# Attention scores on the full array: the low half of k stored twice, and the keys laid out anew

## The chip, the cores and the metric

The kernel runs on one core of one Trainium2 chip. The metric is the device time of one execution in microseconds. Before the change the median of three runs is 2488.95 us (2488.07 to 2495.45).

## The reference, cut to what matters

One inference step of a trunk of two layers, over 128 context tokens and 512 latent tokens on an 8 x 64 grid. Each layer has three mixer branches and a gated feed-forward. Two branches are attention, and the change is in how their scores are computed:

```python
def block_attention(q, k, v):              # branch a: 8 query heads, 2 key/value heads, head width 64
    s = jnp.einsum('bqgrd,bkgd->bgrqk', q_i, k).astype(jnp.float32) * scale
    p = jax.nn.softmax(s, axis=-1)
...
def neighbourhood_attention(q, k, v, kc, vc, rpb):   # branch c: 8 heads, 8 x 16 window
    s_loc = jnp.einsum('bqhd,bqkhd->bhqk', q_i, k_i) * scale + bias_i
    s_ctx = jnp.einsum('bqhd,bchd->bhqc', q_i, kc) * scale
    p = jax.nn.softmax(jnp.concatenate([s_loc, s_ctx], axis=-1), axis=-1)
```

Latent queries of branch a see 512 latent and 128 cached keys; those of branch c see their window and 128 cached keys; context queries see the 128 context keys alone. Branch b is a state-space model (S5).

## The kernel before

Products run in a reduced-width float32 format, and each operand is kept as a high part and a low part, so that a product is a sum of three (high x high, high x low, low x high). Dense products of the hidden state stream 384 or 256 tokens over a stationary 128 x 128 block of weights (`fm_run`, `fm_half`), which come as chunks of 512 KB and are split in two parts by the scalar and the vector engine on the way.

**Scores.** A head is 64 wide and the array takes 128 rows. So `stack` and `evac_q` put the high part of q in one half of the partitions and the low part in the other, and k's high part is stored in both halves. One product over 128 rows then gives (q high + q low) x k high. A second product takes only the 64 partitions that hold q's high part, against k's low part, which is stored once (`klo`): this is a matmul on a row tile of the array. The helper is `scores`.

**Branch a (`gqa_prep`, `gqa`, `gqa_unit`).** For each of four pairs of heads and five tiles of 128 queries, the 640 scores of a head lie in two banks of PSUM, as 512 and 128 columns; with two products each, that is four matmuls per head. Context tiles have one run of 128 keys. `softmax` takes the maximum (vector engine), the exponential (scalar engine) and the scaling (vector engine); then the probabilities are transposed (`transpose_P`, tile `PT`) and multiplied by v (`pv`, tile `y`, two column tiles of 64). The dense products of the gates, the S5 outputs, its gated unit and branch b fill the tensor engine meanwhile.

**Branch c (`neighbourhood`, `na_proj`, `na_pair`).** For each pair of heads, `na_proj` projects q and k and `na_pair` works on blocks 0 to 3 of 128 latent queries and block 4, the context. A latent block has 256 window keys, from two neighbouring tiles of 128, and the 128 cached ones: 256 and 128 columns, two products each, four matmuls per head. The bias is added to the window's scores by the vector engine, the cached keys' scores are copied by the scalar engine, both into `Pn`. Fill comes from the projections of the next pair, branch a's output product, gate c and, in layer 0, the modulation products.

**Order.** The tile framework orders each engine's instructions by what can run first in its own simulated timeline (`schedule_with_timeline_sim=True`); what frees banks is marked `top()`. All DMAs of the kernel are issued by the sync engine (SP), in order.

Of the kernel before, what the change touches and what calls it, by code (L numbers as in the profile page):

```python
# [38 lines left out]
# gates before the S5 outputs; gates of branch c among them; chunks of w_in[u] and of w_up split in halves  # L39
# [4 lines left out]
# chunks of w_out and w_down (8 and 22) kept for the later token tiles; the groups of tiles; the order of the chunks  # L44
# [6 lines left out]
class Trunk:  # L51
# [111 lines left out]
    # ------------------------------------------------------------ weight stream  # L163
# [36 lines left out]
    def ws_early(self, first, n, pool):  # L200
        """Chunks ahead of their turn, for products that start with the tokens of the first half."""
# [6 lines left out]
    def ws_next(self, *key):  # L208
        """The hi and lo parts of the next chunk of weights, which the host lays out by the keys asked for."""
# [15 lines left out]
    # ------------------------------------------------------------ matmul groups  # L225
# [6 lines left out]
    def fm_half(self, out, w, a, K, c, n):  # L232
        """out[128 features, n tokens] = sum over k of w[:, k].T @ a[:, k, c:c+n], in hi/lo parts."""
# [26 lines left out]
    def tm_run(self, name, l, kper, n, evac):  # L260
        """Token-major products of the hidden state with n outputs."""
# [15 lines left out]
    # ------------------------------------------------------------ program  # L277
# [22 lines left out]
    def extra(self):  # L300
        """Three more banks, while the wide scores don't need them."""
# [24 lines left out]
    def setup(self):  # L326
# [20 lines left out]
        # silu of the two conditioning vectors, in the first two of 32 columns  # L347
# [118 lines left out]
    def adaln(self, l, vecs, pool, raw, bank):  # L466
        """silu(c) @ w_mod + b of both conditioning vectors, four tiles of 256 columns side by side on the array."""
# [60 lines left out]
    def tails(self, outs, xt, nxt):  # L528
        """x += gg * rmsnorm(product) of the token tiles; then the norm nxt = (layer, which), or the output."""
# [91 lines left out]
    def out_phase(self, name, K, src, l, which, nxt):  # L621
        """x += gg * rmsnorm(product), and the norm that follows, over groups of token tiles. Of w_out most chunks stay
        for the later groups, and the third tile goes between the others, so that the first three are normed in time
        for the next phase."""
# [47 lines left out]
    # ------------------------------------------------------------ mixer  # L672
# [62 lines left out]
    def gates(self, l, pool):  # L735
        """Gate b, which stays in M, and what of the other two gates is done early and kept in DRAM."""
# [50 lines left out]
    def nv(self, l, VN):  # L787
        """The values of the neighbourhood attention, token-major."""
# [8 lines left out]
    def gate(self, l, b, dst, js=range(8)):  # L797
        """tanh of half the gate logits of one branch."""
# [8 lines left out]
    def br(self, l, b, y, G=None):  # L807
        """merged (times 2) += 2 * sigmoid(gate logits) * (y @ w_br) of one branch; the first finds its gate in M."""
# [17 lines left out]
    # ------------------------------------------------------------ attention  # L826
    def scores(self, out, q, k, klo, r0, qv, kv):
        """q.T @ k of one head: q is stacked (hi at r0, lo in the other half), k is hi twice, klo at r0."""
        self.mm(out, qv(q), kv(k), True, False)
        self.mm(out, qv(q[r0:r0 + 64]), kv(klo[r0:r0 + 64]), False, True)  # L830

    def transpose_P(self, parts, pool, npt):
        """The [128, 128] parts of probabilities, transposed; four at a time."""
# [11 lines left out]
    def softmax(self, P, src, nk):  # L845
        """exp(src - max), divided by its sum, of two heads."""
        m, sm, r = (self.st([128, 2], x) for x in ("mx", "sm", "rc"))
        for hh in range(2):
            c = slice(hh, hh + 1)
            self.nc.vector.tensor_reduce(out=m[:, c], in_=src[hh], axis=AX.X, op=ALU.max, negate=True)  # L850
            self.act(P[:, hh, :nk], src[hh], AF.Exp, bias=m[:, c], accum=sm[:, c])
# [3 lines left out]
    def pv(self, tiles, pt, v):  # L855
        """probabilities.T @ v of two heads side by side on the array."""
# [13 lines left out]
    def gqa_prep(self, l, pool, p_y, zt):  # L870
# [7 lines left out]
        ckt = tab[:, 4, 384:512]  # L878
        self.dma(g.rearrange("p a d -> p (a d)"), A["qkg"][l].to_broadcast([128, 128]))
        kst = self.kst = pool.tile([128, 3, 768], R, tag="kst", name="kst")  # L880
        self.dma(ckt, A["ckt"][l])
# [28 lines left out]
        klo = kst[:, 2]  # L910
        parts = [(x[:, :n], c, n) for x, c, n in b] + [(ckt, 640, 128)]
        for b, c, n in parts:
            for kv in range(2):
                r = slice(kv * 64, kv * 64 + 64)
                for o in (0, 64):
                    self.act(kst[o:o + 64, kv, c:c + n], b[r])
                self.sub(klo[r, c:c + n], b[r], kst[r, kv, c:c + n].bitcast(F))
# [10 lines left out]
    def stack(self, pool, zt, p):  # L928
        """q of the two heads of pair p, stacked hi/lo, times 1/8."""
# [10 lines left out]
    def gqa_unit(self, pool, p_sc, p, t, q, va):  # L940
        """Two query heads of one pair, 128 queries: softmax over 640 keys (latents) or 128 (context)."""
        kv = p // 2
        k, klo = self.kst[:, kv], self.kst[:, 2]
# [3 lines left out]
        for hh in range(2):  # L947
            sc.append(p_sc.tile([128, 1024], F, tag="sc", name="sc"))
            for a, b in ((0, 512), (512, 640)) if t else ((0, 128),):
                c0 = a + (128 if t else 0)  # L950
                self.scores(sc[hh][:, a:b], q[:, hh], k, klo, 64 * kv, qv, lambda x: x[:, c0:c0 + b - a])
        P = pool.tile([128, 2, 640], F, tag="P", name="P", bufs=2)
        self.softmax(P, [x[:, :nk] for x in sc], nk)
# [5 lines left out]
    # ------------------------------------------------------------ neighbourhood attention  # L959
# [25 lines left out]
    def na_pair(self, pool, yc, p, ops):  # L985
        """Two heads, 128 queries: blocks 0..2 are grid columns 8+16b.., block 3 the outer 8 + 8 columns, 4 the context."""
        q, kk, bias, _, _ = ops
        k, klo = (kk[:, 0], kk[:, 1]), kk[:, 2]
        for b in (4, 0, 1, 2, 3):
# [4 lines left out]
            def kv(x):  # L994
                if b == 3:
                    return x[:, 128:640].rearrange("p (u v) -> p u v", v=128)[:, 0::3, :]
                return x[:, 128 + 128 * b:384 + 128 * b]

            P = pool.tile([128, 2, 384], F, tag="P", name="Pn", bufs=2)
            for hh in range(2):  # L1000
                sc = self.tq() if (5 * hh + b) % 3 == 0 else self.px()
                if b < 4:
                    self.scores(sc[:, 0:256], q[hh], k[hh], klo, hh * 64, qv, kv)
                c0 = 0 if b == 4 else 640
                self.scores(sc[:, nk - 128:nk], q[hh], k[hh], klo, hh * 64, qv, lambda x: x[:, c0:c0 + 128])
                if b < 4:
                    v = lambda x: x.rearrange("p (g r c) -> p g r c", g=4, r=8)
                    bb = bias[:, hh, 1 if b == 3 else 0, :].rearrange("p (r g c) -> p g r c", r=8, g=4)
                    self.add(v(P[:, hh, 0:256]), v(sc[:, 0:256]), bb)
                self.act(P[:, hh, nk - 128:nk], sc[:, nk - 128:nk])  # L1010
# [3 lines left out]
            tiles = {4: [0], 3: [1, 4, 5]}.get(b, [b + 1, b + 2, 5])  # L1014
# [8 lines left out]
    def na_bias(self, l):  # L1023
        """Relative bias of the two kinds of query block, laid out by query: [128, 8 heads, 8 rows x 32 columns]."""
# [554 lines left out]
```

## Time and profile before

| | |
|---|---|
| runs | 2488.07, 2488.95, 2495.45 us |
| span of the profiled execution | 2490.8 us |
| tensor engine busy | 2430.1 us (98%), 16154 matmuls |
| weight loads busy | 2140.1 us (86%) |
| vector engine busy | 1483.9 us (60%) |
| scalar engine busy | 1229.6 us (49%) |
| mean granted clock of the tensor engine | 0.991 |

The profile gives no time for its execution apart from the span, which lies 1.9 us above the median of the runs. Matmuls overlap in their pipeline and their ends are modelled: a matmul's duration reads about 0.16 us longer than the distance to the next one's start. What a matmul costs is therefore read from start to start in the timeline. A line of the timeline joins neighbouring instructions of one name, shows the shape of the first, and xN is their count; "128\*128" is rows x columns of the array that are used, "64\*128" is a row tile, "128x384" is rows x streamed columns.

### The profile page before, as it was taken

The page shows a single profiled execution, that of the slowest core. Times are in us where ns is not written, and L with a number is a line of the kernel's source. Part 1 is how long each engine was busy: PE and PEld are TensorE (multiplying, and loading weights), DVE is VectorE, ACT ScalarE, POOL GpSimd, SP SyncE. Part 2 cuts the span into 40 slices and gives each one's busy share as a digit, 9 for nine tenths or more (in the row PEclk, how much of TensorE's full clock was granted, in tenths as well). Part 3 has the DMA queues.
Part 4 walks back from the last instruction along what each step waited for, and adds up shares of the span by engine and source line. Part 5 has one row for each costly group of instructions (what it writes and reads, how often), then busy time and mean ns, then how long its engine had stood idle before and what let it go on. Part 6 is the DMA issues. An engine that isn't in the chain of part 4 may idle for free.

```text
span 2490.8 us, 41473 instructions
## 1 busy us (share of the span) xinstructions
PE 2430.1 (98%) x16154; PEld 2140.1 (86%) x16154; DVE 1483.9 (60%) x3269; ACT 1229.6 (49%) x2679; POOL 0.7 (0%) x6
## 2 busy tenths in 40 slices
PE   5999999999999999999999999999999999999998
PEld 4888887878788888999888988888888899999886
DVE  8788536355456866665474684463654665444446
ACT  5434675345536544344465447754455364444434
POOL 0000000000000000000000000000000000000000
PEclk8999999999999999999999999999999999999999
DMA  7862342444224567654456313413211432222335
GB/s 262 276 209 80 107 142 57 138 133 152 86 90 147 193 218 229 215 174 142 156 189 197 106 60 121 134 47 120 86 50 53 147 121 89 73 72 77 127 110 178
DMA packets 158510, 333.91 MB, mean 134 GB/s; under 512 B 38954, under 2 KB 71530, under 8 KB 158314
## 3 DMA queue, kind: packets, MB, share of 16 engines
q1 hardware_dynamic: 158314, 331.26, 40.7%
q8 instruction: 127, 2.08, 0.4%
q14 instruction: 69, 0.57, 0.1%
HBM read 288.05 MB, written 52.53 MB: 137 GB/s over the span
## 4 chain that ended last, share of the span: by engine, by line
PE 93%; DMA 2%; ACT 2%; DVE 2%; issue 1%; SPq 0%; DVEq 0%; ACTq 0%
PE mm L227 52%; PE m L227 16%; PE mx L227 9%; PE tq L227 4%; PE sc L227 3%; PE y L227 3%; PE PT L230 3%; DMA wm<-in_wmod 1%; PE E L227 1%; DMA ar<-in_wmod 1%; PE BT L230 1%; DMA raw<-in_wst 0%; PE xT L230 0%; DVE lo L99 0%; ACT h L130 0%
## 5 line engine op out<-in xcount | busy, mean ns | idle before, releaser
L227 PE MATMUL mm<-h,hi 128*128 128x384 f32 (+1 forms) x3808 | 866.1, 315 | 7.2 <-ACT h L130 4.1
L227 PEld LDWEIGHTS mm<-h,hi 128*128 128x128 f32 x3808 | 642.6, 190 | 29.8 <-issue 15.9
L227 PE MATMUL mm<-h,lo 128*128 128x384 f32 (+1 forms) x1904 | 594.7, 312 | 0.0
L99 DVE TENSOR_TENSOR lo<-raw,hi 128x1024 fp32r<-128x1024 f32 x294 | 359.6, 1224 | 309.8 <-ACT hi L130 307.0
L130 ACT ACTIVATE hi<-raw 128x1024 fp32r<-128x1024 f32 x294 | 310.9, 1058 | 311.9 <-PE mm L227 214.0
L227 PEld LDWEIGHTS mm<-h,lo 128*128 128x128 f32 x1904 | 361.8, 190 | 4.7 <-issue 3.7
L227 PE MATMUL m<-h,hi 128*128 128x256 f32 (+1 forms) x1120 | 250.8, 313 | 1.8 <-ACT vn L130 1.1
L227 PEld LDWEIGHTS m<-h,hi 128*128 128x128 f32 x1120 | 188.4, 190 | 8.0 <-issue 4.6
L227 PE MATMUL m<-h,lo 128*128 128x256 f32 (+1 forms) x560 | 174.3, 311 | 0.1
L130 ACT ACTIVATE PT<-PT 128x512 f32<-128x512 f32 (+1 forms) x176 | 87.0, 499 | 122.0 <-PE PT L230 97.2
L117 DVE SCALAR_TENSOR_TENSOR c<-u,blob,c 128x641 f32<-128x641 f32 x156 | 137.9, 884 | 2.2
L227 PEld LDWEIGHTS m<-h,lo 128*128 128x128 f32 x560 | 106.3, 190 | 2.7 <-issue 2.2
L130 ACT ACTIVATE u<-mm 128x256 f32<-128x256 f32 (+1 forms) x156 | 48.1, 344 | 113.0 <-PE mm L227 113.0
L227 PE MATMUL sc<-kst,qst 64*128 64x128 f32 (+3 forms) x288 | 96.6, 387 | 0.0
L227 PE MATMUL mm<-a,hi 128*128 128x384 f32 (+1 forms) x384 | 89.9, 321 | 2.1 <-DVE a L117 1.3
L227 PEld LDWEIGHTS sc<-kst,qst 128*128 128x128 f32 (+1 forms) x288 | 53.3, 185 | 40.5 <-issue 33.9
L850 DVE TENSOR_REDUCE mx<-sc 128x1 f32<-128x640 f32 (+1 forms) x80 | 57.2, 716 | 44.7 <-PE sc L227 44.1
L130 ACT ACTIVATE HK<-a 64x32 f32<-64x32 f32 (+1 forms) x256 | 77.2, 335 | 12.8 <-PE mm L227 10.3
L227 PE MATMUL mm<-hi,sph 128*128 128x512 f32 x208 | 78.5, 392 | 1.4 <-ACT sph L130 1.4
L227 PE MATMUL mm<-lo,sph 128*128 128x512 f32 x208 | 78.5, 391 | 0.0
L99 DVE TENSOR_TENSOR pr<-PW,cS 128x576 f32<-128x576 f32 x64 | 47.8, 754 | 51.4 <-PE mx L227 32.3
L227 PE MATMUL mm<-set,hi 128*128 128x384 f32 (+1 forms) x324 | 76.6, 320 | 0.3 <-DVE a L117 0.3
(357 smaller groups left out, 4393.6 us busy)
## 6 DMA issues: line engine op xcount, KB each, us to landing
raw<-in_wst SPq DMA_DIRECT2D x308, 512.0 KB
ar<-in_wmod SPq DMA_DIRECT2D x80, 512.0 KB
cd<-pr SPq DMA_DIRECT2D x32, 288.0 KB
v<-cd SPq DMA_DIRECT2D x32, 288.0 KB
wm<-in_wmod SPq DMA_DIRECT2D x8, 1024.0 KB
xd<-xt SPq DMA_DIRECT2D x15, 512.0 KB
xt<-xd SPq DMA_DIRECT2D x15, 512.0 KB
bd<-BT SPq DMA_DIRECT2D x28, 256.0 KB
```

Of the source, the lines that this page charges most:

```text
L99: return self.nc.vector.tensor_tensor(out=out, in0=a, in1=b, op=op)
L117: self.nc.vector.scalar_tensor_tensor(out=out, in0=a, scalar=s, in1=b, op0=op0, op1=op1)
L130: return self.nc.scalar.activation(out=out, in_=a, func=func, **kw)
L227: return self.nc.tensor.matmul(out=out, lhsT=lhsT, rhs=rhs, start=start, stop=stop)
L230: return self.nc.tensor.transpose(out, in_, self.ident)
L850: self.nc.vector.tensor_reduce(out=m[:, c], in_=src[hh], axis=AX.X, op=ALU.max, negate=True)
```

## The change

The low part of k is stored in both halves of the partitions, as the high part is, so that both products of a score go over 128 rows. (The second product then adds q low x k low too.) The 640 keys of a latent tile in branch a are taken as two runs of 320, one per bank. In branch c the cached keys stand twice among the latent ones, at columns 384 and 768, so that the 384 keys of any block are one run (block 3: three pieces at a stride), with one matmul per product; v's tiles are taken in the same order, and the bias add of blocks 1 and 3 is cut in two because the cached keys stand in the middle. The cached keys are loaded by four DMAs instead of one, into both halves; in branch a they land in a part of the table that also serves as scratch for the rotary, and later in the program. The softmax reads the scores of branch a as two runs of 320. The tiles grow, and a scratch size of the program is lowered (every DMA of this kernel goes by SP's queue).

```diff
-    def scores(self, out, q, k, klo, r0, qv, kv):
+    def scores(self, out, q, k, klo, qv, kv):
         self.mm(out, qv(q), kv(k), True, False)
-        self.mm(out, qv(q[r0:r0 + 64]), kv(klo[r0:r0 + 64]), False, True)
+        self.mm(out, qv(q), kv(klo), False, True)
...
# gqa_prep
-        ckt = tab[:, 4, 384:512]
+        ck2 = tab[:, 4, 0:256].rearrange("p (a k) -> p a k", a=2)
-        kst = self.kst = pool.tile([128, 3, 768], R, tag="kst", name="kst")
-        self.dma(ckt, A["ckt"][l])
+        kst = self.kst = pool.tile([128, 4, 768], R, tag="kst", name="kst")
...
         b = self.transposed(zt, 512, self.tq)
-        klo = kst[:, 2]
-        parts = [(x[:, :n], c, n) for x, c, n in b] + [(ckt, 640, 128)]
-        for b, c, n in parts:
+        for kv in range(2):
+            for o in (0, 64):
+                self.dma(ck2[o:o + 64, kv], A["ckt"][l][kv * 64:kv * 64 + 64])
+        for b, c, n in b:
             for kv in range(2):
                 r = slice(kv * 64, kv * 64 + 64)
                 for o in (0, 64):
-                    self.act(kst[o:o + 64, kv, c:c + n], b[r])
-                self.sub(klo[r, c:c + n], b[r], kst[r, kv, c:c + n].bitcast(F))
+                    hi, lo = (kst[o:o + 64, i + kv, c:c + n] for i in (0, 2))
+                    self.act(hi, b[r, :n])
+                    self.sub(lo, b[r, :n], hi.bitcast(F))
+        hi, lo = (kst[:, i:i + 2, 640:768] for i in (0, 2))
+        self.act(hi, ck2)
+        self.sub(lo, ck2, hi.bitcast(F))
...
# gqa_unit
-            for a, b in ((0, 512), (512, 640)) if t else ((0, 128),):
-                c0 = a + (128 if t else 0)
-                self.scores(sc[hh][:, a:b], q[:, hh], k, klo, 64 * kv, qv, lambda x: x[:, c0:c0 + b - a])
+            for a, c0, n in ((0, 128, 320), (512, 448, 320)) if t else ((0, 0, 128),):
+                self.scores(sc[hh][:, a:a + n], q[:, hh], k, klo, qv, lambda x: x[:, c0:c0 + n])
...
# na_pair
+                self.scores(sc[:, 0:nk], q[hh], kk[:, hh], kk[:, 2 + hh], qv, kv)
+                cc = 0 if b == 4 else 128 if b % 2 else 256
                 if b < 4:
-                    self.scores(sc[:, 0:256], q[hh], k[hh], klo, hh * 64, qv, kv)
-                c0 = 0 if b == 4 else 640
-                self.scores(sc[:, nk - 128:nk], q[hh], k[hh], klo, hh * 64, qv, lambda x: x[:, c0:c0 + 128])
...
+                    for c0, g0, ng in ((0, 0, 2), (256, 2, 2)) if b % 2 else ((0, 0, 4),):
+                        v = lambda x: x[:, c0:c0 + 64 * ng].rearrange("p (g r c) -> p g r c", g=ng, r=8)
+                        self.add(v(P[:, hh]), v(sc), bb[:, g0:g0 + ng])
...
# na_proj
-        self.dma(ckt, self.A["cknt"][l, p])
+        for hh in range(2):
+            for o in (0, 64):
+                self.dma(ck2[o:o + 64, hh], self.A["cknt"][l, p][hh * 64:hh * 64 + 64])
...
+            c += 128 * half
             for hh in range(2):
-                r, o = slice(hh * 64, hh * 64 + 64), slice(64 - hh * 64, 128 - hh * 64)
-                self.act(k[hh][r, c:c + n], src[r])
-                self.act(k[hh][o, c:c + n], src[r])
-                self.sub(klo[r, c:c + n], src[r], k[hh][r, c:c + n].bitcast(F))
...
+                for o in (0, 64):
+                    hi, lo = (kk[o:o + 64, i + hh, c:c + n] for i in (0, 2))
+                    self.act(hi, ps[hh * 64:hh * 64 + 64])
+                    self.sub(lo, ps[hh * 64:hh * 64 + 64], hi.bitcast(F))
...
-                put_k(ckt, 640, 128)
+                for c in (384, 768):
+                    hi, lo = (kk[:, i:i + 2, c:c + 128] for i in (0, 2))
+                    self.act(hi, ck2)
+                    self.sub(lo, ck2, hi.bitcast(F))
```

## Rows read from the trace of the kernel before

**Rows 1.** The page: span, busy time of each engine, chain by engine.

```profile
span 2490.8 us, 41473 instructions
PE 2430.1 (98%) x16154; PEld 2140.1 (86%) x16154; DVE 1483.9 (60%) x3269; ACT 1229.6 (49%) x2679; POOL 0.7 (0%) x6
...
PE 93%; DMA 2%; ACT 2%; DVE 2%; issue 1%; SPq 0%; DVEq 0%; ACTq 0%
```

**Rows 2.** Windows 205:455, 500:745, 1440:1710 and 1735:1965, summed.

```profile
sum 995.00, PE 981.99 PEld 838.72 DVE 560.78 ACT 534.37 POOL 0.00; mean PE 245.50 PEld 209.68 DVE 140.20 ACT 133.59 POOL 0.00
```

**Rows 3.** Timeline of PE: four scores of branch a, dense on both sides.

```profile
413.07 1.33 PE L227 MATMUL sc<-kst,qst 128*128 128x512 f32 x4
414.34 0.50 PE L227 MATMUL mm<-a,hi 128*128 128x256 f32 x2
414.68 0.28 PE L227 MATMUL mm<-a,lo 128*128 128x256 f32 x1
```

**Rows 4.** Timeline of PE: eight scores of branch c, two heads of a block.

```profile
525.13 1.10 PE L227 MATMUL mx<-set 128*128 128x256 f32 x4
...
527.30 0.44 PE L227 MATMUL mm<-set,hi 128*128 128x384 f32 x1
527.58 0.34 PE L227 MATMUL mm<-set,lo 128*128 128x384 f32 x1
```

**Rows 5.** Timeline of PE: scores of a context tile, two heads.

```profile
250.34 1.09 PE L227 MATMUL sc<-kst,qst 128*128 128x128 f32 x4
251.36 0.44 PE L227 MATMUL mm<-h,lo 128*128 128x384 f32 x1
```

**Rows 6.** Timeline of PE: dense products without a break.

```profile
2203.31 0.51 PE L227 MATMUL mm<-h,hi 128*128 128x384 f32 x2
...
2207.48 0.40 PE L227 MATMUL mm<-h,hi 128*128 128x256 f32 x2
...
2210.34 0.52 PE L227 MATMUL m<-h,hi 128*128 128x384 f32 x2
```

**Rows 7.** Timeline of PE: single scores among dense products, full and row-tiled.

```profile
1801.85 0.22 PE L227 MATMUL mx<-set 128*128 128x128 f32 x1
1801.91 0.39 PE L227 MATMUL m<-h,hi 128*128 128x384 f32 x1
1802.13 0.33 PE L227 MATMUL m<-h,lo 128*128 128x384 f32 x1
...
1802.66 0.34 PE L227 MATMUL m<-h,lo 128*128 128x384 f32 x1
1802.93 0.32 PE L227 MATMUL mx<-set 64*128 64x128 f32 x1
1803.18 0.61 PE L227 MATMUL m<-h,hi 128*128 128x384 f32 x2
1803.63 0.34 PE L227 MATMUL m<-h,lo 128*128 128x384 f32 x1
```

**Rows 8.** Timeline of the weight loads: the first row tile of Rows 3.

```profile
413.40 0.18 PEld L227 LDWEIGHTS sc<-kst,qst 64*128 64x128 f32 x1 [0.31 <-issue]
```

**Rows 9.** The page's groups: weight loads of the dense products.

```profile
L227 PEld LDWEIGHTS mm<-h,hi 128*128 128x128 f32 x3808 | 642.6, 190 | 29.8 <-issue 15.9
```

**Rows 10.** Groups by form on DVE: operations of the kinds that the change adds.

```profile
L99 DVE TENSOR_TENSOR set<-mm,set 64x384 fp32r<-64x384 f32 x16 | 8.9, 555 | 16.5 <-ACT set L130 16.2
L99 DVE TENSOR_TENSOR set<-mm,set 64x256 fp32r<-64x256 f32 x12 | 5.0, 419 | 1.7 <-ACT set L130 1.5
L99 DVE TENSOR_TENSOR set<-sf,set 64x128 fp32r<-64x128 f32 x16 | 4.5, 283 | 1.9 <-ACT set L130 1.4
```

**Rows 11.** Window in which layer 1's q and k of branch a are prepared.

```profile
1410.00:1445.00 35.00, 35.00 (x241) 34.87 (x240) 31.99 (x102) 15.02 (x34) 0.00 (x0) 1.00 0.25 78
```

**Rows 12.** What the SP queue waited for longest: us in total, times, longest.

```profile
SPq L136 <- DVE lo L99: 858.6, 188, 19.7
```

**Rows 13.** Tile sf: issues of the cached keys, ns min/median/max.

```profile
L136 SPq DMA_DIRECT2D sf<-in_cknt x8: 327/328/424, 483.5 to 1832.0; - x8
```

More of the change, by code (lines that the diff above doesn't have):

```diff
@@ L849, in softmax @@
             c = slice(hh, hh + 1)
-            self.nc.vector.tensor_reduce(out=m[:, c], in_=src[hh], axis=AX.X, op=ALU.max, negate=True)
-            self.act(P[:, hh, :nk], src[hh], AF.Exp, bias=m[:, c], accum=sm[:, c])
+            wide = len(src[hh].shape) == 3
+            self.nc.vector.tensor_reduce(out=m[:, c], in_=src[hh], axis=AX.XY if wide else AX.X, op=ALU.max, negate=True)
+            o = P[:, hh, :nk]
+            self.act(o.rearrange("p (b c) -> p b c", b=2) if wide else o, src[hh], AF.Exp, bias=m[:, c],
+                     accum=sm[:, c])
             self.nc.vector.reciprocal(out=r[:, c], in_=sm[:, c])
@@ L942, in gqa_unit @@
         kv = p // 2
-        k, klo = self.kst[:, kv], self.kst[:, 2]
+        k, klo = self.kst[:, kv], self.kst[:, 2 + kv]
         nk = 640 if t else 128
@@ L948, in gqa_unit @@
             sc.append(p_sc.tile([128, 1024], F, tag="sc", name="sc"))
-            for a, b in ((0, 512), (512, 640)) if t else ((0, 128),):
-                c0 = a + (128 if t else 0)
-                self.scores(sc[hh][:, a:b], q[:, hh], k, klo, 64 * kv, qv, lambda x: x[:, c0:c0 + b - a])
+            for a, c0, n in ((0, 128, 320), (512, 448, 320)) if t else ((0, 0, 128),):
+                self.scores(sc[hh][:, a:a + n], q[:, hh], k, klo, qv, lambda x: x[:, c0:c0 + n])
         P = pool.tile([128, 2, 640], F, tag="P", name="P", bufs=2)
-        self.softmax(P, [x[:, :nk] for x in sc], nk)
+        self.softmax(P, [x.rearrange("p (b c) -> p b c", b=2)[:, :, :320] if t else x[:, :128] for x in sc], nk)
         pt = self.transpose_P([P[:, hh, kt * 128:kt * 128 + 128] for kt in range(nk // 128) for hh in range(2)], pool, 2)
@@ L987, in na_pair @@
         q, kk, bias, _, _ = ops
-        k, klo = (kk[:, 0], kk[:, 1]), kk[:, 2]
         for b in (4, 0, 1, 2, 3):
@@ L995, in kv @@
                 if b == 3:
-                    return x[:, 128:640].rearrange("p (u v) -> p u v", v=128)[:, 0::3, :]
-                return x[:, 128 + 128 * b:384 + 128 * b]
+                    return x[:, 128:896].rearrange("p (u v) -> p u v", v=128)[:, 0::2, :]
+                c0 = (128, 256, 512, 0, 0)[b]
+                return x[:, c0:c0 + nk]
             P = pool.tile([128, 2, 384], F, tag="P", name="Pn", bufs=2)
@@ L1001, in na_pair @@
                 sc = self.tq() if (5 * hh + b) % 3 == 0 else self.px()
+                self.scores(sc[:, 0:nk], q[hh], kk[:, hh], kk[:, 2 + hh], qv, kv)
+                cc = 0 if b == 4 else 128 if b % 2 else 256
                 if b < 4:
-                    self.scores(sc[:, 0:256], q[hh], k[hh], klo, hh * 64, qv, kv)
-                c0 = 0 if b == 4 else 640
-                self.scores(sc[:, nk - 128:nk], q[hh], k[hh], klo, hh * 64, qv, lambda x: x[:, c0:c0 + 128])
-                if b < 4:
-                    v = lambda x: x.rearrange("p (g r c) -> p g r c", g=4, r=8)
                     bb = bias[:, hh, 1 if b == 3 else 0, :].rearrange("p (r g c) -> p g r c", r=8, g=4)
-                    self.add(v(P[:, hh, 0:256]), v(sc[:, 0:256]), bb)
-                self.act(P[:, hh, nk - 128:nk], sc[:, nk - 128:nk])
+                    for c0, g0, ng in ((0, 0, 2), (256, 2, 2)) if b % 2 else ((0, 0, 4),):
+                        v = lambda x: x[:, c0:c0 + 64 * ng].rearrange("p (g r c) -> p g r c", g=ng, r=8)
+                        self.add(v(P[:, hh]), v(sc), bb[:, g0:g0 + ng])
+                self.act(P[:, hh, cc:cc + 128], sc[:, cc:cc + 128])
             self.softmax(P, [P[:, hh, :nk] for hh in range(2)], nk)
@@ L1013, in na_pair @@
             pt = self.transpose_P([P[:, hh, i * 128:i * 128 + 128] for i in range(n) for hh in range(2)], pool, 3)
-            tiles = {4: [0], 3: [1, 4, 5]}.get(b, [b + 1, b + 2, 5])
+            tiles = ([1, 2, 5], [2, 5, 3], [3, 4, 5], [1, 5, 4], [0])[b]
             o = self.pv(tiles, pt, lambda vt, hh: self.VN[:, vt, (2 * p + hh) * 64:(2 * p + hh) * 64 + 64])
@@ L1037, in na_tiles @@
     def na_tiles(self, i, pool, dt=R):
-        return (pool.tile([128, 3840], R, tag=f"set{i}", name="set"),
-                pool.tile([128, 1280], dt, tag=f"sf{i}", name="sf"))
+        return (pool.tile([128, 4992], R, tag=f"set{i}", name="set"),
+                pool.tile([128, 1408], dt, tag=f"sf{i}", name="sf"))
     def na_operands(self, p, pool):
         t, f = self.na_tiles(p % 2, pool, F)
-        kk = t[:, 0:2304].rearrange("p (i c) -> p i c", i=3)
-        q = [t[:, 2304 + i * 704:3008 + i * 704] for i in range(2)]
-        return q, kk, f[:, 0:1024].rearrange("p (h i k) -> p h i k", h=2, i=2), f[:, 1024:1152], f[:, 1152:1280]
+        kk = t[:, 0:3584].rearrange("p (i c) -> p i c", i=4)
+        q = [t[:, 3584 + i * 704:4288 + i * 704] for i in range(2)]
+        ck2 = f[:, 1024:1280].rearrange("p (h k) -> p h k", h=2)
+        return q, kk, f[:, 0:1024].rearrange("p (h i k) -> p h i k", h=2, i=2), ck2, f[:, 1280:1408]
     def na_parts(self, i, pool):
-        t, f = (x.rearrange("p (i k c) -> p i k c", i=2, c=NT) for x in self.na_tiles(i, pool))
+        t, f = (x[:, :n].rearrange("p (i k c) -> p i k c", i=2, c=NT)
+                for x, n in zip(self.na_tiles(i, pool), (3840, 1280)))
         return lambda k: [t[:, i, k] if k < 3 else f[:, i, 0] for i in range(2)]
     def na_proj(self, l, p, ops):
-        q, kk, bias, ckt, kc = ops
-        k, klo = (kk[:, 0], kk[:, 1]), kk[:, 2]
-        self.dma(ckt, self.A["cknt"][l, p])
+        q, kk, bias, ck2, kc = ops
+        for hh in range(2):
+            for o in (0, 64):
+                self.dma(ck2[o:o + 64, hh], self.A["cknt"][l, p][hh * 64:hh * 64 + 64])
         for kind in range(2):
@@ L1066, in evac_q, with evac_k @@
                     self.stt(q[hh][o, d:d + w], src, 0.125, hi.bitcast(F), ALU.mult, ALU.subtract)
-        def put_k(src, c, n):
+        def evac_k(half, ps, c, n):
+            c += 128 * half
             for hh in range(2):
-                r, o = slice(hh * 64, hh * 64 + 64), slice(64 - hh * 64, 128 - hh * 64)
-                self.act(k[hh][r, c:c + n], src[r])
-                self.act(k[hh][o, c:c + n], src[r])
-                self.sub(klo[r, c:c + n], src[r], k[hh][r, c:c + n].bitcast(F))
-        def evac_k(half, ps, c, n):
-            put_k(ps, c, n)
+                for o in (0, 64):
+                    hi, lo = (kk[o:o + 64, i + hh, c:c + n] for i in (0, 2))
+                    self.act(hi, ps[hh * 64:hh * 64 + 64])
+                    self.sub(lo, ps[hh * 64:hh * 64 + 64], hi.bitcast(F))
             if half == 0:
@@ L1560 @@
     from concourse.bass_utils import run_bass_kernel_spmd
-    nc = bacc.Bacc("TRN2", target_bir_lowering=False, num_devices=1)
+    nc = bacc.Bacc("TRN2", target_bir_lowering=False, num_devices=1, dynamic_dma_scratch_size=1024)
     A = {k: nc.dram_tensor(f"in_{k}", v, F, kind="ExternalInput").ap() for k, v in INS.items()}
```

## Prediction

> **What bounds the kernel now.** I read the page first: the tensor engine (PE) is busy 98% of a span of 2490.8 us and holds 93% of the chain that ended last [rows 1]. An average over stages could hide a stage that waits for something else, so I then read the windows of the four stretches in which attention runs (branch a and branch c, in both layers). Together they last 995 us, and PE is busy in 982 of them, the vector engine (DVE) in 561 and the scalar engine (ACT) in 534 [rows 2]. So in the stretches of the change too, PE is what ends last: 13 us of idle time in all. A busy PE is not yet a PE at its rate, so the third view is the timeline of PE, read from one start to the next, for the price of a product there.
>
> **What a dense product costs.** In an unbroken stretch, 24 products of 384 columns take 2207.48 - 2203.31 = 4.17 us, 174 ns each, and the 24 of 256 columns after them 2.86 us, 119 ns each [rows 6].
>
> **What scores cost now.** Four scores of one head in branch a (512 columns on the full array, 512 on a row tile, 128 full, 128 row-tiled) take 414.34 - 413.07 = 1.27 us, and the two dense products after them 0.34 us where two take 0.24: the group costs 1.37 us [rows 3]. Its 1280 columns would take about 0.58 us at the dense rate. In branch c, two heads of a block (1536 columns) take 2.17 us, and the dense product after them 0.28 us for 0.17: 2.28 us [rows 4]. Two heads of a context tile (512 columns) take 1.02 us [rows 5].
>
> **Why, as far as rows tell.** Two single scores of 128 columns stand between dense products [rows 7]. The full one is over after 0.06 us, and the dense product behind it takes 0.22 us for 0.17: about 0.11 us in all. The row-tiled one takes 0.25 us, the dense product ahead of it 0.27 us for 0.17, the one behind it about 0.10 us too much: 0.45 us. So a matmul of few columns isn't dear; passing into a row tile and out of it is, about 0.34 us for the round trip. The loads agree: ahead of the row tile's weights the load unit stands still 0.31 us, with nothing to wait for but issue [rows 8], whereas dense loads have 29.8 us of idle time over 3808 [rows 9].
>
> The Trainium skill, "TensorEngine Tiling (Array Packing)", section Key Properties, says that changing the tiling mode drains the engine; that is what these rows look like, and the change removes such a passage in every score. By another page the sum comes out otherwise; it is a rival below.
>
> **The sum.** Per layer and pair there are four latent tiles or blocks with two heads each: 2 x 4 x 4 x 2 = 64 head groups in each branch, and 8 context units of two heads in each.
>
> - Branch a: four full products of 320 columns. No row shows 320; it lies between 119 and 174 ns, and I take 147. So 1.37 becomes 0.59 us: -0.78 x 64 = -50 us (bounds -43 and -57).
> - Branch c: four full products of 384 columns for two heads: 2.28 becomes 0.70 us: -1.58 x 32 = -51 us.
> - Context: four full products of 128 columns at 0.06 to 0.11 us: 1.02 becomes 0.34 us: -0.68 x 16 = -11 us.
>
> That is 112 us if each group stood alone between dense products. Not all do: groups of different heads already run into each other, and a group followed by a transpose or by a product with v has no cheap neighbour to make cheap again. I take off 10 us, an estimate (bounds 0 and 25): 102 us.
>
> **What it adds.** On DVE, per pair in branch c: two more subtractions of 64x384 and two of 64x256, 2 x 0.555 + 2 x 0.419 = 1.95 us; for the cached keys two of 256 columns in place of two of 128, +0.27 us [rows 10]. Eight pairs: 18 us. The cut bias add is two operations of 128 columns for one of 256, +0.15 us in two blocks, two heads, eight pairs: 5 us. Preparing branch a's keys takes two more subtractions of 512 columns, about 0.69 us each by the step between 256 and 384 [rows 10], and two of 128, less one operation on the cached keys: some 2 us in each layer, 4 in all. So DVE has about 27 us more work; ACT has a little less (one operation for four on branch a's cached keys, two for four in branch c). In the four stretches DVE then has some 588 of about 893 us, 66%, for 56% now: PE's dense products hide it. Without that cover it costs up to 27 us. Two places have thin cover. One is the preparation of branch a in layer 1, where DVE is busy 31.99 of 35 us while PE runs without a gap [rows 11]; gates are the cover, and all 4 us would show without them. The other is the evacuation of k's projection: its bank is held by four subtractions where there were two, 1.1 us longer, with the next-but-one product waiting for it.
>
> **DMAs.** The cached keys are four issues for one: at 0.33 us each [rows 13], 1 us more of SP's time in ten places, and twice as many bytes of a small transfer. In branch a these loads now wait for the rotary's scratch to be free, which they didn't, and weight chunks queue behind them on SP. SP mostly waits for buffers anyway (858.6 us for the weight splits, 19.7 us the longest [rows 12]), and three chunks are split ahead, each worth 24 x (0.174 + 0.119) = 7.0 us of PE [rows 6]. I cost it at nothing; it costs 0 to 10 us. The scratch size, the order of v's tiles and the three-piece keys of block 3 I cost at nothing: same bytes, same counts.
>
> **What is late next.** With scores shorter, each unit's softmax chain starts earlier, but its maximum, exponential, scaling and transposes are as long as before, and fill is used up by the microsecond that the scores no longer take. PE's 13 us of idle time in these stretches [rows 2] should grow. I add 8 us, about two thirds of what is there; from below it is 0, from above about the added DVE work, 27 us.
>
> Sum: 2490.8 - 102 + 8 = 2397 us of span. The median of the runs lies 1.9 us under the profiled span, so the forecast is **2395 us**.
>
> **Rivals.**
> 1. *Waits eat a part* (20%): DVE's 27 us land on PE's path, through banks of k's projection and softmax chains, and the fill that the planner sets aside for the end of a branch is used up too early, about one chunk of 7 us in each of two branches and two layers. 2395 - 8 + 27 + 28 - 2 = about 2440; in part, 2410 to 2440. For it: DVE at 32 of 35 us in one stretch [rows 11]. Against it: 434 us of idle DVE in the four stretches [rows 2].
> 2. *Loads of the full array don't hide* (3%): each of the 448 new products shows its weight load of 190 ns [rows 9] beyond its columns. 448 x 0.19 = 85 us come back: 2480. The Trainium skill, "TensorE: Matmul & The Clock Gate", Part 3, states such a rule: loads overlap matmuls in flight only where the row group differs, which speaks against leaving row tiles. The trace disagrees with it: dense products on all rows go at 119 ns with loads of 190 ns [rows 6, 9], and the load that does not overlap is the row tile's [rows 8].
> 3. *The row tile isn't the cause* (2%): a score keeps its gap of about 0.2 us because of its operands. Branch a keeps its time, as it keeps its four products; in branch c four matmuls become two, 64 x 2 x 0.2 = 26 us: 2463. The lone full score at 0.06 us speaks against it [rows 7].
> 4. *The SP queue* (3%), slower than before: the late loads of cached keys hold up the weight stream behind them in branch a's preparation and at each projection. Ten places; the gain of 94 us is gone once each stops PE for 9.4 us, so from waits of 21 + 9.4 = 30 us on, three chunks being ahead. At 31 us each: 2395 + 104 = 2499. Against it: SP's longest wait is 19.7 us [rows 12].
>
> **How the numbers follow.** The forecast's own case has 72%, with 2376 to 2410: a gain of 112 us and no new waits gives 2377, and 25 us of neighbours that stay dear gives 2410. To hold 8 in 10, the range takes in the part of rival 1 up to 2435: 2377 to 2435, about 15 to 20% left out at both ends. A difference of 0.3%, 7.5 us, is about what a measurement of this kernel can tell from none. Faster: the forecast, rivals 1, 2 (2480 is 0.36% under 2488.95) and 3, less a tail: 95%. Slower: rival 4, 3%. Within 0.3%: 2%.
>
> **What would show it.** In the profile after: no row-tiled score; scores of branch a as four products in 0.59 us between dense ones, of branch c as 174 ns each; no 0.31 us of idle load unit ahead of them; 128 matmuls fewer; PE's busy time down by about 100 us with its share near 97 or 98%; DVE's busy time up by about 27. It would be wrong if full products of scores stood more than about 0.2 us apart, or if idle time of PE rose by tens of microseconds in the four stretches, with DVE or a weight chunk as what ended it.

## The result, and the profile after

The changed kernel takes 2423.75 us, median of four runs (2418.54 to 2427.51), against 2489.18 us (2488.07 to 2495.45): a ratio of 0.9734, 95% interval 0.9717 to 0.9750. It is faster by 65 us where 94 were forecast, and lies inside the range.

The page of the profile after, to be held against [rows 1]:

```profile
span 2416.8 us, 41307 instructions
...
PE 2334.5 (97%) x16026; PEld 2103.6 (87%) x16026; DVE 1501.8 (62%) x3339; ACT 1221.7 (51%) x2657; POOL 0.7 (0%) x6
...
PE 85%; DMA 4%; ACT 4%; DVE 3%; issue 1%; SPq 0%; DVEq 0%; ACTq 0%
```

The tensor engine has 128 matmuls fewer and is busy 2430.1 - 2334.5 = 95.6 us less. But the span fell by only 74.0 us, because the time in which that engine is not busy grew from 2490.8 - 2430.1 = 60.7 to 82.3 us. Its share of the chain fell from 93% to 85%. The clock is not the reason: its mean granted value is 0.990 in this execution, for 0.991 before.

The scores themselves cost what the sum said. Timeline of PE, eight scores of branch a (two heads, 320 columns each) between dense products, to be held against [rows 3]:

```profile
220.88 1.34 PE L227 MATMUL sc<-kst,qst 128*128 128x320 f32 x8
222.06 0.28 PE L227 MATMUL mm<-h,hi 128*128 128x256 f32 x1
222.17 0.28 PE L227 MATMUL mm<-h,lo 128*128 128x256 f32 x1
```

From 220.88 to 222.06 is 1.18 us for eight, 147 ns each, and the dense product behind them takes 0.11 us, no more than its usual 0.12. Timeline of PE, two heads of a block in branch c, to be held against [rows 4]: first between dense products, then behind four transposes.

```profile
1706.86 0.52 PE L227 MATMUL mx<-set 128*128 128x384 f32 x2
1707.21 0.51 PE L227 MATMUL tq<-set 128*128 128x384 f32 x2
1707.56 0.28 PE L227 MATMUL m<-set,hi 128*128 128x256 f32 x1
...
1782.39 0.65 PE L230 MATMUL PT<-ident,Pn 128*128 128x128 f32 x4
1782.81 0.59 PE L227 MATMUL tq<-set 128*128 128x384 f32 x2
1783.24 0.51 PE L227 MATMUL mx<-set 128*128 128x384 f32 x2
1783.59 0.28 PE L227 MATMUL mm<-h,lo 128*128 128x256 f32 x1
```

The first four take 0.70 us, 174 ns each; the ones behind transposes take 0.78. A passage stays, then, of about 0.08 us behind a transpose. It is of the kind for which the forecast took 10 us off. The loads of eight scores now run without a gap (timeline of the weight loads, to be held against [rows 8]):

```profile
220.76 1.19 PEld L227 LDWEIGHTS sc<-kst,qst 128*128 128x128 f32 x8
```

What is new is idle time. The windows over the four stretches of attention after, to be held against [rows 2]:

```profile
205.00:455.00 250.00, 242.71 (x1816) 222.97 (x1815) 150.59 (x416) 154.96 (x376) 0.00 (x0) 0.99 0.33 108
465.00:695.00 230.00, 215.20 (x1533) 182.78 (x1532) 139.28 (x330) 108.35 (x285) 0.00 (x0) 0.98 0.37 123
1410.00:1650.00 240.00, 232.46 (x1746) 214.79 (x1745) 145.32 (x392) 153.61 (x371) 0.00 (x0) 0.99 0.31 102
1660.00:1870.00 210.00, 206.22 (x1446) 188.19 (x1445) 137.03 (x321) 117.09 (x302) 0.00 (x0) 1.00 0.24 75
sum 930.00, PE 896.59 PEld 808.73 DVE 572.22 ACT 534.00 POOL 0.00; mean PE 224.15 PEld 202.18 DVE 143.05 ACT 133.50 POOL 0.00
```

The columns after the length are PE, PEld, DVE, ACT and POOL, busy us and instructions. The tensor engine stands still 33 us of 930, where it was 13 of 995; the largest part, 14.8 us, is in branch c of layer 0. The view of waits names who ended the waits that are new or longer, over the whole program (us in total, times, longest):

```profile
PE m L227 <- DMA ar<-in_wmod: 6.6, 7, 1.5
...
PE y L227 <- ACT PT L130: 4.2, 7, 1.1
PE sc L227 <- ACT P L130: 4.1, 6, 1.7
...
PE tq L227 <- ACT set L130: 2.4, 4, 1.0
...
PE mx L227 <- ACT set L130: 1.8, 4, 0.5
```

In the same view of the kernel before, neither ACT P nor ACT set ends a wait of the tensor engine, and the first two rows are shorter:

```profile
PE y L227 <- ACT PT L130: 1.6, 3, 0.6
PE m L227 <- DMA ar<-in_wmod: 1.6, 3, 0.7
```

### The profile page after: what moved, and what is told of

It is laid out like the page before. It is cut to its first block, busy times and chain, and to the rows that moved or that the text cites. A ratio compares the mean times of both kernels' runs of the same rounds, so it can differ in the third digit from the quotient of the medians.

```text
span 2416.8 us, 41307 instructions
## 1 busy us (share of the span) xinstructions
PE 2334.5 (97%) x16026; PEld 2103.6 (87%) x16026; DVE 1501.8 (62%) x3339; ACT 1221.7 (51%) x2657; POOL 0.7 (0%) x6
## 4 chain that ended last, share of the span: by engine, by line
PE 85%; DMA 4%; ACT 4%; DVE 3%; issue 1%; SPq 0%; DVEq 0%; ACTq 0%
PE mm L227 49%; PE m L227 16%; PE mx L227 7%; PE tq L227 4%; PE y L227 3%; PE PT L230 2%; DMA ar<-in_wmod 2%; PE sc L227 1%; DMA raw<-in_wst 1%; ACT HK L130 1%; DVE lo L99 1%; PE BT L230 1%; ACT h L130 1%; PE E L227 1%; DMA cd<-pr 1%
## 5 line engine op out<-in xcount | busy, mean ns | idle before, releaser
L227 PE MATMUL mm<-h,hi 128*128 128x384 f32 (+1 forms) x3808 | 855.8, 313 | 6.3 <-ACT h L130 4.1
L227 PE MATMUL mm<-hi,spl 128*128 128x512 f32 x208 | 73.2, 393 | 0.0
L130 ACT ACTIVATE c<-u,blob 128x641 f32<-128x641 f32 x78 | 72.2, 925 | 1.9
L227 PEld LDWEIGHTS mm<-a,hi 128*128 128x128 f32 x384 | 63.9, 190 | 7.5 <-ACT a L130 4.1
```

Source lines behind the costliest of these rows:

```text
L130: return self.nc.scalar.activation(out=out, in_=a, func=func, **kw)
L227: return self.nc.tensor.matmul(out=out, lhsT=lhsT, rhs=rhs, start=start, stop=stop)
```

## The experiments

Medians are given with the ratio to the kernel before, measured on the same chip, and its 95% interval. The changed kernel is at 0.9734 [0.9717, 0.9750].

**e1_old_cut: full array, but the columns cut as before.**

```diff
-            for a, c0, n in ((0, 128, 320), (512, 448, 320)) if t else ((0, 0, 128),):
+            for a, c0, n in ((0, 128, 512), (512, 640, 128)) if t else ((0, 0, 128),):
...
-                self.scores(sc[:, 0:nk], q[hh], kk[:, hh], kk[:, 2 + hh], qv, kv)
+                for c0, c1 in ((0, 256), (256, 384)) if b < 4 else ((0, 128),):
...
+                    self.scores(sc[:, c0:c1], q[hh], kk[:, hh], kk[:, 2 + hh], qv, kc)
```

> The changed kernel with every product on 128 rows as now, but the columns cut as before the change: 512 and 128 in branch a, 256 and 128 in branch c, so the count of matmuls is as before. Theory (the passage into row tiles was the whole cost): a head of branch a takes 2 x 229 + 2 x 60 to 110 = 0.58 to 0.68 us where it now takes 0.59, a head of branch c 2 x 119 + 2 x 60 to 110 = 0.36 to 0.46 us for 0.35; 128 heads make +0 to +13 us on 2424, so 2424 to 2437. Rival (narrow products of 128 columns are dear by themselves, 0.257 us as in the old groups): 256 of them at +0.15 to 0.2 us give +38 to +51 us, 2462 to 2475.

Measured: 2424.29 us, 0.9734 [0.9714, 0.9754]. The same as the changed kernel. The new runs of 320 and 384 columns, for which branch c's keys were reordered, bring nothing that this measurement can tell. The tensor engine is busy 2347.5 us for 2334.5, 0.1 us for each of the 128 products more, and stands still 5 us less. The narrow products of 128 columns were never dear.

**e2_row_tiles_back: the new layout and all its copies, the second product back on 64 rows.**

```diff
-        self.mm(out, qv(q), kv(klo), False, True)
+        self.mm(out, qv(q[r]), kv(klo[r]), False, True)      # r: the 64 rows of q's high part
```

> The changed kernel with its new layout and all its added copies, but the second product of each score back on 64 rows. Theory (each stay on a row tile costs a round trip of 0.34 us, 0.2 into and out of each product in a run): 128 such products in branch a, 64 in branch c, 32 in the context units: 224 x 0.34 = +76 us, less some where two row tiles follow each other: 2424 + 60 to 76 = 2484 to 2500. Rival (the row tile is not the cause, the layout of the keys in fewer and equal runs is): 2424 to 2440.

Measured: 2486.47 us, 0.9983 [0.9970, 0.9995]. Of 65 us, 63 go back with this one operand. The tensor engine is busy 2412.6 us, 78 us more than in the changed kernel, where 224 round trips of 0.34 us are 76. The profile shows where. Eight scores of branch a take 2.61 us from start to start, for 1.18 (timeline of PE):

```profile
220.24 2.68 PE L227 MATMUL sc<-kst,qst 128*128 128x320 f32 x8
222.85 0.38 PE L227 MATMUL mm<-h,hi 128*128 128x256 f32 x1
```

And the groups by form on PE of this kernel:

```profile
L227 PE MATMUL sc<-kst,qst 64*128 64x320 f32 x128 | 53.7, 420 | 0.0
...
L227 PE MATMUL sc<-kst,qst 128*128 128x320 f32 x128 | 49.6, 388 | 1.3 <-ACT P L130 1.2
```

The two products of a score, full and row-tiled, read 0.39 and 0.42 us in the mean, where in the changed kernel the mean is 0.319 over all 256:

```profile
L227 PE MATMUL sc<-kst,qst 128*128 128x320 f32 x256 | 51.0, 319 | 3.8 <-ACT P L130 3.7
```

So the row tile was the cause, and the full product ahead of it pays as well.

**e4_low_twice: the added subtractions done twice.**

```diff
-                    self.sub(lo, ps[hh * 64:hh * 64 + 64], hi.bitcast(F))
+                    for _ in range(1 if o == 64 * hh else 2):
+                        self.sub(lo, ps[hh * 64:hh * 64 + 64], hi.bitcast(F))
```

(and likewise in branch a.)

> The changed kernel with the subtractions for the second copy of k's low part done twice: as much vector engine work once more as the change adds for k, about 16 us in branch c and 4 us in branch a, on banks held about 1 us longer. Theory A (the part of the gain that went missing is idle time from chains and fill, not the added vector work): +0 to +5 us, 2424 to 2429. Theory B (the added vector work lands on the tensor engine's path): +13 to +20 us, 2437 to 2444.

Measured: 2422.48 us, 0.9728 [0.9710, 0.9746]. The vector engine is busy 1520.6 us for 1501.8, and the time doesn't move. The amount of vector work is not what ate the gain. The scalar engine's waits for the vector engine on k grow as well, to 13.7 us for 10.2 in the changed kernel (view of waits).

**e6_scratch: the kernel before with the smaller scratch alone.**

```diff
-    nc = bacc.Bacc("TRN2", target_bir_lowering=False, num_devices=1)
+    nc = bacc.Bacc("TRN2", target_bir_lowering=False, num_devices=1, dynamic_dma_scratch_size=1024)
```

> The kernel before the change, with the scratch size lowered as in the change and nothing else. All theories: no difference, 2489 within 4 us; if it moves by more, part of the change's result is not from the scores.

Measured: 2491.50 us, 1.0000 [0.9985, 1.0014]. The scratch size makes no difference.

**e5_two_ar and e7_high_first: two ways to take away new idle time.** The first gives the modulation weights beside branch c two buffers:

```diff
-                raw = lambda k: p_na.tile([128, 1024], F, tag="ar", name="ar", bufs=1)
+                raw = lambda k: p_na.tile([128, 1024], F, tag="ar", name="ar", bufs=2)
```

> The changed kernel with two buffers in place of one for the modulation weights that run beside branch c of layer 0 (the tile ar). In the profile after, the tensor engine stands still 6.6 us there for the landing of ar, for 1.6 us before. Theory A (that idle time is real loss): -4 to -6 us, about 2419, and that releaser near 0. Theory B (the planner only moves the wait elsewhere): 2424 within 2 us.

Measured: 2418.54 us, 0.9712 [0.9695, 0.9729]; the wait for ar falls from 6.6 to 2.7 us, but that of tq for ACT set grows from 2.4 to 4.4. The time is what theory A asked for, but the interval overlaps that of the changed kernel: inconclusive.

The second writes k's high parts first:

```diff
-            for hh in range(2):
-                for o in (0, 64):
-                    hi, lo = (kk[o:o + 64, i + hh, c:c + n] for i in (0, 2))
-                    self.act(hi, ps[hh * 64:hh * 64 + 64])
-                    self.sub(lo, ps[hh * 64:hh * 64 + 64], hi.bitcast(F))
+            parts = [(hh, [kk[o:o + 64, i + hh, c:c + n] for i in (0, 2)]) for hh in range(2) for o in (0, 64)]
+            for hh, (hi, lo) in parts:
+                self.act(hi, ps[hh * 64:hh * 64 + 64])
+            for hh, (hi, lo) in parts:
+                self.sub(lo, ps[hh * 64:hh * 64 + 64], hi.bitcast(F))
```

(and likewise for the cached keys and in branch a.)

> The changed kernel with all four high parts of k written first and all four low parts after them (the two engines write the same tile in turns as the change has it, and each waits for the other). Theory A (the longer chain of turns holds up the first scores of a pair and is part of the new idle time, 3.6 us in layer 0): that releaser falls to near 0, and the time by 3 to 6 us, about 2419. Theory B (dense products would have filled it, what is lost is lost to the shorter scores): 2424 within 2 us.

Measured: 2404.51 us, 0.9656 [0.9639, 0.9673], 19 us less, far more than theory A asked for. The timelines show what the order did. The changed kernel, first half of k of the first pair, ACT and DVE, and the score on PE that waits for it:

```profile
479.77 0.48 ACT L130 ACTIVATE set<-mm 64x384 fp32r<-64x384 f32 x1 [3.04 <-PE mm L227]
480.28 0.55 DVE L99 TENSOR_TENSOR set<-mm,set 64x384 fp32r<-64x384 f32 x1 [3.10 <-ACT set L130]
480.87 0.48 ACT L130 ACTIVATE set<-mm 64x384 fp32r<-64x384 f32 x1 [0.62 <-DVE set L99]
481.38 0.55 DVE L99 TENSOR_TENSOR set<-mm,set 64x384 fp32r<-64x384 f32 x1 [0.55 <-ACT set L130]
481.97 0.49 ACT L130 ACTIVATE set<-mm 64x384 fp32r<-64x384 f32 x1 [0.62 <-DVE set L99]
482.49 0.56 DVE L99 TENSOR_TENSOR set<-mm,set 64x384 fp32r<-64x384 f32 x1 [0.55 <-ACT set L130]
483.32 1.06 ACT L130 ACTIVATE hi<-raw 128x1024 fp32r<-128x1024 f32 x1 [0.87 <-PE mm L227]
...
484.97 0.48 ACT L130 ACTIVATE set<-mm 64x384 fp32r<-64x384 f32 x1
...
485.50 0.33 PE L227 MATMUL tq<-set 128*128 128x128 f32 x1 [0.75 <-ACT set L130]
...
486.31 1.01 DVE L99 TENSOR_TENSOR set<-mm,set 64x384 fp32r<-64x384 f32 x2
```

The same place in e7_high_first:

```profile
481.66 1.99 ACT L130 ACTIVATE set<-mm 64x384 fp32r<-64x384 f32 x4 [2.76 <-PE mm L227]
483.68 2.28 DVE L99 TENSOR_TENSOR set<-mm,set 64x384 fp32r<-64x384 f32 x4 [4.33 <-ACT set L130]
```

In turns, each engine waits 0.55 to 0.62 us for the other; the fourth high part, which the first score of the second head needs (485.50), starts 5.2 us after the first one, behind a weight split that got in between, and its subtraction at 486.31, 6.5 us after the start (the line joins it with one of the second half). With the high parts first all eight operations are over in 4.3 us, and the fourth high part starts 1.5 us after the first. In the kernel before there were two turns, two high parts in each, and the fourth started 2.1 us after the first (timeline of ACT):

```profile
503.95 0.98 ACT L130 ACTIVATE set<-mm 64x384 fp32r<-64x384 f32 x2 [2.32 <-PE mm L227]
505.55 0.99 ACT L130 ACTIVATE set<-mm 64x384 fp32r<-64x384 f32 x2 [0.62 <-DVE set L99]
```

**e8_both: the two together.**

> Both edits of e5_two_ar and e7_high_first. Theory A: -8 to -12 us, 2412 to 2416. Theory B: 2424 within 2 us.

Measured: 2404.92 us, 0.9657 [0.9639, 0.9674]: as e7_high_first alone. Beside the new order the second buffer gains nothing that this measurement can tell.

**e10_before_high_first: the same order in the kernel before.**

```diff
-            for hh in range(2):
-                r, o = slice(hh * 64, hh * 64 + 64), slice(64 - hh * 64, 128 - hh * 64)
-                self.act(k[hh][r, c:c + n], src[r])
-                self.act(k[hh][o, c:c + n], src[r])
-                self.sub(klo[r, c:c + n], src[r], k[hh][r, c:c + n].bitcast(F))
+            for hh, r in enumerate(rs):
+                for o in rs[hh], rs[1 - hh]:
+                    self.act(k[hh][o, c:c + n], src[r])
+            for hh, r in enumerate(rs):
+                self.sub(klo[r, c:c + n], src[r], k[hh][r, c:c + n].bitcast(F))
```

(and likewise in branch a.)

> The kernel before the change with all high parts of k written first and the low parts after them, as in e7_high_first. Theory A (the change doubled the turns that the two engines take on one tile, and that is what e7_high_first gave back): before it there were half as many turns, and dense products covered them, so little is gained, 0 to -5 us on 2489. Theory B (writing the high parts first is worth some 19 us to any version, so it explains nothing about the change): about 2470.

Measured: 2493.93 us, 1.0013 [1.0003, 1.0023]. No gain, rather 3 us of loss, just outside what theory A gave. The old order cost nothing before the change. But it also had less to give there: the fourth high part came 2.1 us after the first, and comes 1.5 us after it in this run.

**e12_high_first_c: the order in branch c alone.**

> e7_high_first in branch c alone (eight places); branch a's k (two places) in turns as the change has it. If branch c's k is what cost: 2405 to 2410, near e7_high_first. If the two preparations of branch a, where the vector engine is 90% busy, cost most: 2415 to 2420.

Measured: 2407.99 us, 0.9664 [0.9648, 0.9681]. Most of it, 17 of the 19 us by the ratios, is branch c's k.

**e13_low_apart: branch c's low parts in a tile of their own, the order as in the change.**

```diff
+                pool.tile([128, 1792], R, tag=f"low{i}", name="low"))
...
-                    hi, lo = (kk[o:o + 64, i + hh, c:c + n] for i in (0, 2))
+                    hi, lo = (x[o:o + 64, hh, c:c + n] for x in kk)
```

> The changed kernel with k's low parts of branch c in a tile of their own, written in the order of the change (a high part, its low part, the next high part). Theory A (the turns come of both engines writing one tile): the scalar engine's waits for the vector engine on k, 10.2 us in the changed kernel, go, and the time falls as in e12_high_first_c, to 2405 to 2412. Theory B (the turns come of the order, high and low part by part out of one bank of PSUM, whichever tile they go to): the waits stay near 10 us, and the time within 4 us of 2424.

Measured: 2421.65 us, 0.9725 [0.9702, 0.9747], and the waits stay. The view of waits of e13_low_apart:

```profile
ACT set L130 <- DVE low L99: 10.5, 18, 1.9
```

of the changed kernel:

```profile
ACT set L130 <- DVE set L99: 10.2, 18, 1.6
```

and of the kernel before:

```profile
ACT set L130 <- DVE set L99: 4.7, 8, 0.6
```

Theory A of this run falls: it is not the common tile. The wait goes with the order in which the two engines take their parts, and in e7_high_first no such row is listed. That the bank they share is the reason is what is left, but no run takes the parts out of two banks. One more row speaks for it: in e7_high_first the vector engine starts at 483.68, when the fourth high part is done, though the first one, all that its first subtraction needs, was done 1.5 us earlier.

**e9_states_shared and e11_q_high_first: further.** The first adds to e8_both that half of the S5 state copies go to the vector engine:

```diff
-                        self.act(dst[:, :, 0:16], hv[:, :, 15::-1])
-                        self.act(dl, lat[:, :, ::-1, ::-1])
+                        self.cpy(dst[:, :, 0:16], hv[:, :, 15::-1])
+                        self.cpy(dl, lat[:, :, ::-1, ::-1])
```

> e8_both, and half of the copies of the S5 states (tile HK, 256 copies, 77 us on the scalar engine) moved to the vector engine. In branch a the scalar engine is busy some 80% of the stretch of the S5 outputs, and scores and products with v wait for its exponentials and copies. If that engine's queue is what ends those waits: idle time of the tensor engine in branch a falls from 7 us per layer to 3 or 4, -5 to -8 us against e8_both, about 2407. If the copies on the vector engine only hold up the maxima there: no gain or up to 5 us more.

Measured: 2397.06 us, 0.9623 [0.9606, 0.9641], 8 us less than e8_both; the scalar engine is busy 1183.4 us for 1219.8 there. The size is what was expected, the mechanism only in part: the tensor engine's idle time in 240 us of branch a falls from 5.6 to 2.5 us in layer 1, but from 8.0 only to 7.6 in layer 0. Where the rest of the 8 us comes from is not shown.

The second adds q's high parts first, in both branches:

> e9_states_shared with q's high parts first as well, in both branches (the two engines take turns on q's tile too, in all versions so far; the profile of the changed kernel has the scalar engine waiting 12.8 us for the vector engine there). If turns are dear wherever they stand: -3 to -8 us against 2397, about 2391. If q's turns are covered by the dense products of k that come next: 2397 within 2 us.

Measured: 2398.30 us, 0.9626 [0.9609, 0.9642]. No further gain, though the waits of ACT for q's low parts, 8.9 us in e9_states_shared, are no longer listed: those turns cost nothing here.

The best version is e9_states_shared, 92 us under the kernel before and 27 under the changed one.

## Why the prediction was right, and where its size was off

- *What bounds the kernel, and what a row tile costs*: right. The round trip read from two single scores [rows 7] is the whole change: e2_row_tiles_back gives 63 of 65 us back, with 78 us of the tensor engine, and e1_old_cut nothing. The row of 0.06 us for a lone full product had already told that narrow products are cheap.
- *The sum, 102 us of the tensor engine*: 95.6 us measured. The price of 320 columns, put at 147 ns in the middle of two bounds, is 147 ns. The 128 columns of the context's scores, put at 0.06 to 0.11 us, mostly go at 0.11 us in the trace after, 2 us more in all than the sum took.
- *The added work*: the durations of the vector engine's operations, added up from each trace, rise from 1623.3 to 1650.7 us, by 27 us as forecast. Its busy time rises by 1501.8 - 1483.9 = 18 us only, as neighbouring operations overlap and busy time counts the overlap once. e4_low_twice shows that as an amount this work costs nothing.
- *What is late next, 8 us*: this is the term that was mis-sized. Idle time of the tensor engine grew by 82.3 - 60.7 = 21.6 us in the profiled execution, 20 of them in the four stretches. A part of it is the evacuation of k, which was costed as "1.1 us longer, with the next-but-one product waiting for it". I counted four subtractions and missed the order: high and low part by part, the scalar engine waits for each subtraction, 18 times and 10.2 us for 8 times and 4.7 us before, and the last high part comes late. Writing the high parts first gives 19 us back in the changed kernel and none in the one before.
- *How the order comes to cost 19 us* is argued, not shown. Between the two profiled executions, e7_high_first has 9.9 us less idle time of the tensor engine (72.4 for 82.3) and 4.3 us less busy time, and the rows in which that engine waits for parts of k or q (ACT set) hold 4.2 us in all, and are gone there. The length of the scalar engine's waits does not go with the time: they are 13.7 us in e4_low_twice, which is no slower. What does go with it is how late the fourth high part comes. In the four pairs of layer 0, first half, it starts 2.1 us after the first one before the change, 5.2 to 6.4 us after the change, 5.2 to 7.0 us in e4_low_twice, and 1.5 us in e7_high_first and e12_high_first_c. With the order mended, 72.4 - 60.7 = 11.7 us of new idle time are left, near the 8 forecast. Every edit also lets the framework order all engines anew. That this alone made the gain is unlikely: the three kernels with branch c's high parts first and nothing moved between engines lie at 2404.5 to 2408.0, the five with the old order and no row tile at 2418.5 to 2424.3.
- *Profile and median*: the profiled execution of the changed kernel, at 2418.54 us, was the fastest of its four; the median lies 7 us above its span, where the forecast took 1.9 us below. Each run's time is about 1.8 us above its own span, so this is no more than which execution was profiled: before the change one of about 2492.6 us, above its median. The three differences, 6.4 + 13.6 + 8.9, make the 29 us between 2395 and 2424, and the last of them is chance.
- *The rivals*: the first, waits that eat a part, is what happened in part, by the banks of k's projection as it said, though not by the amount of vector work. Loads that don't hide are refuted: eight loads follow each other without a gap in 1.19 us, beside eight products at 147 ns each. The Trainium skill, "TensorE: Matmul & The Clock Gate", Part 3, has loads overlap matmuls in flight only where the row group differs; the trace of the changed kernel disagrees, by those rows. That the row tile is not the cause is refuted by e2_row_tiles_back. The SP queue did not stop the stream of chunks: no load of a chunk stands among the waits of the tensor engine that the view lists, and the queue's longest wait is 20.2 us. (This rival's price was added wrong: ten waits of 31 us, 21 of them covered, make 100 us and 2495, not 2499.)
- *The signs*: those on row tiles, on the price of a score, on the loads, on the count of matmuls and on the tensor engine came as said. Of the two that were to show the forecast wrong, one came half true: idle time rose by 20 us in the four stretches, but what ended the new waits was the scalar engine and the modulation weights, not the vector engine or a chunk.
- *Still open*: why layer 0's branch c keeps more idle time than layer 1's, 14.8 for 3.8 us in the windows above. Two buffers for ar didn't settle it, and no run takes the modulation products out of that stretch.

## What to carry to other kernels

Price a matmul from start to start, together with its neighbour on each side: what looks like a dear product may be a passage between shapes of the array, and one lone instance among dense products tells them apart. When an edit adds copies to an evacuation, write out the order in which the two engines will read the bank, not only the sum of their work. And when an engine gets faster by a few per cent, expect the order of the others to be what is late next, and look for it in who waits for whom.

## What the runs showed of the hardware that was not expected

The full product beside a row tile pays as much as the row tile itself: in e2_row_tiles_back the eight scores of branch a go at 0.33 us each, for 0.147 us with all on the full array, and the two kinds read 0.388 and 0.420 us in the mean, for 0.319. A transpose ahead of a full score costs 0.08 us as well, less than a row tile does. And the scalar and the vector engine, which evacuate one bank part by part, wait out each other's work: 0.62 us for a subtraction of 0.55, 0.55 us for a copy of 0.48, whichever tile they write. The view names the other engine's instruction as what ended such a wait; whether the chip would need the wait, no run shows.
